# Encoder step on one core: the down projection's operands fetched by product, copied in pairs and subtracted on GpSimd, with spills laid out by pairs

## The chip, the cores and the metric

The kernel runs on one core of a Trainium2 chip. The metric is the device time of one execution in microseconds (us); lower is better. Times of before are the median of three runs.

## The reference, cut to what matters

One layer of a streaming encoder is computed for 592 tokens (16 meta tokens, 512 prompt frames, 64 sample frames): attention in two head groups, an output projection with a residual, and then the part that the change touches, a SwiGLU feed-forward network with a residual and a final norm, in float32, with D_MODEL = 2048 and D_FF = 5632:

```python
x = x + mix @ lp['w_out']
h = rmsnorm(x, lp['norm_ffn_g'])
x = x + (jax.nn.silu(h @ lp['ffn_w_gate']) * (h @ lp['ffn_w_up'])) @ lp['ffn_w_down']
...
y_prompt = rmsnorm(xp[:, N_META:], final_norm_g)
```

## The kernel before

Activations lie transposed: 128 features on the partitions, the 576 tokens that are kept as two halves of QH = 288 columns. Each float32 operand is split in two (`split`, L155): ScalarE (ACT) copies it to a rounded `hi` and VectorE (DVE) subtracts to get `lo`. A product is then three matmuls, hi x hi, hi x lo (both L1089) and lo x hi (L1093).

The feed-forward products run by Strassen-Winograd (`winograd`, L1031): a 2 x 2 block product takes seven products of block sums instead of eight. A *pair* is two chunks of 128 features, so with the two token halves it has four quarters; the seven right-hand operands of a pair are quarters or sums of quarters. For each of the seven products `lhs` (L1067) makes the weight side: products 1, 2 and 4 split a quarter of the raw weights; 5 and 7 need a sum made on GpSimd (POOL), 6 and 3 one made on DVE from an earlier sum (L1058). `split_weights` gives `wh` (ACT, L156) and `wl` (DVE, L153), two buffers each. TensorE (PE) runs the matmuls of all pairs of a block, `take` adds the product to the output on DVE, and `step` lets other work in.

*Gate and up.* 22 turns `u`, each with a gate and an up product over all eight slots of operands (L1243). After each turn GpSimd multiplies the two results (L1278) and, for the first 20 pairs, makes the four sums (L1284 to L1287). The act chunks go to DRAM in `actspill`, the sums in `sumspill`; the DMAs are issued by SP (`load`, `store`).

*Down.* The 22 pairs are taken in blocks of 4, 4, 4, 4, 4 and 2 (L1238). The first five run seven products in the order of `CHAIN` (1, 5, 6, 2, 7, 3, 4) for each of eight turns `d` of 256 output columns; the last runs without sums (`plain_rows`). The output `y` stays in SBUF (16 tiles of 128x576), is first loaded with the residual from `x2spill`, and each product is added to a quarter of it (L1328). While a block runs, `builder` (L1191) prepares the next block's operands in the other four of the eight slots: `fetch` loads a quarter or a sum (144 KB) into `lo`, four loads ahead; ACT copies it to `hi` (L1218), DVE subtracts in place (L1220). Each `step`, so each product, takes one of these two operations: 56 in a block of 56 products. The operands come pair by pair, seven of one pair after another. A separate builder, `start`, prepares the first block at the end of gate/up, by product, and all its copies stand ahead of the first down turn in ACT's program.

Order: SP, ACT, DVE, POOL and PE each run their own queue in order. A scheduler arranges each queue by when it thinks an instruction is ready, except that what `pin` marks (L977, from L1389 on) keeps its place in the program; loads are not marked.

Of the kernel before, what the change touches and what calls it, by code (L numbers as in the profile page):

```python
# [19 lines left out]
P = 128  # L20
# [95 lines left out]
def encoder_step(  # L116
# [195 lines left out]
    x2spill = dp.tile([KC, P, TQ], F32, name="x2spill")  # L312
    actspill = dp.tile([FC, P, TQ], F32, name="actspill")
    sumspill = dp.tile([FC // 2, P, 4, QH], F32, name="sumspill")
# [667 lines left out]

    def operand(m, p, src):
        hi = bc.tile([P, QH], F32R, name=f"bh{p}_{m}")
        lo = bc.tile([P, QH], F32R, name=f"bl{p}_{m}")
        pin(S.activation(hi, src, AF.Copy))
        pin(V.tensor_tensor(lo, src, f32(hi), op=ALU.subtract))
        operands[m, p] = (hi, lo)
# [128 lines left out]
    for i in range(KC):  # L1117
        x = ma.tile([P, TQ], F32, name="x", tag="x", bufs=3)
        load(x, x1spill[i])
        ps = [pmt()[:, 0:QH] for _ in range(2)]  # L1120
        for hf in range(2):
            wh, wl = ws.pop(2 * i + hf)
            for k in range(4):
                mm3(ps, wh[:, k, :], wl[:, k, :],
                    halves(mixh[4 * hf + k]), halves(mixl[4 * hf + k]), hf + k == 0, hf + k == 4)
            fetch(2 * i + hf + 2)
        for xi, pi in zip(halves(x), ps):
            V.tensor_tensor(xi, xi, pi, op=ALU.add)
        xg = ma.tile([P, TQ], F32, name="xg", tag="xg", bufs=2)
        S.activation(xg, x, AF.Copy, scale=gF[:, i:i + 1])  # L1130
        if i == 0:
            G.tensor_tensor(sq2, x, x, op=ALU.mult)
        else:
            G.tensor_tensor(rb2, x, x, op=ALU.mult)
            G.tensor_tensor(sq2, sq2, rb2, op=ALU.add)
        store(x2spill[i], x)
        if i % 2:
            for _ in token_operands(ma, i // 2, xe, xg):
                pass
        xe = xg  # L1140
        if i == 2:
            raw0 = load_raw(rw, w_gate, 0, 8, 0, 1)
# [48 lines left out]
    def builder(m0, count, plain, ahead, by_product=False):  # L1191

        srcs = {}
        for m in range(m0, m0 + count):
            quarter = [actspill[2 * m + f, :, c] for f in range(2) for c in (slice(0, QH), slice(QH, TQ))]
            if plain:
                for p, src in zip((1, 2, 4, 5), quarter):
                    srcs[m, p] = src
            else:
                for p, src in zip(ORDER, (quarter[0], quarter[2], sumspill[m, :, 2], sumspill[m, :, 0],  # L1200
                                          sumspill[m, :, 1], quarter[3], sumspill[m, :, 3])):
                    srcs[m, p] = src
        order = [p for p, _ in CHAIN]
        todo = sorted(srcs, key=lambda mp: order.index(mp[1])) if by_product else list(srcs)

        def fetch(n):
            for m, p in todo[n:n + 1]:
                hi = bc.tile([P, QH], F32R, name=f"bh{p}_{m % 8}")
                lo = bc.tile([P, QH], F32R, name=f"bl{p}_{m % 8}")
                load(f32(lo), srcs[m, p])  # L1210
                operands[m % 8, p] = (hi, lo)

        for n in range(ahead):
            fetch(n)
        for n, (m, p) in enumerate(todo):
            fetch(n + ahead)
            hi, lo = operands[m % 8, p]
            pin(S.activation(hi, f32(lo), AF.Copy))  # L1218
            yield
            pin(V.tensor_tensor(lo, f32(lo), f32(hi), op=ALU.subtract))  # L1220
            yield
# [20 lines left out]
    start = builder(0, blocks[0], False, 4, True)  # L1242
    for u in range(FC // 2):  # L1243
        out = {}
        for which, wsrc in (("g", w_gate), ("u", w_up)):
# [12 lines left out]
            def step():  # L1258
                if u == 0 and which == "u":
                    next(norm, None)  # L1260
                if u == FC // 2 - 1 and which == "u":
                    done[0] += 1
                    if done[0] > 2:
                        for _ in range(2 * blocks[0]):
                            next(start, None)
# [11 lines left out]
        for f in range(2):  # L1277
            G.tensor_tensor(w[:, f, :], w[:, f, :], g[:, f, :], op=ALU.mult)  # L1278
            if u < FC // 2 - 1:
                store(actspill[2 * u + f], w[:, f, :])  # L1280
        if u < FC // 2 - blocks[-1]:
# [6 lines left out]
            store(sumspill[u], t)  # L1288
    for _ in start:
        pass  # L1290
    for f in range(2):
        store(actspill[FC - 2 + f], out["u"][:, f, :])
# [8 lines left out]
    def plain_rows(m0, n, d, hs, slots, done):  # L1301
# [13 lines left out]
        for f in range(2):  # L1315
            for h in hs:
                c = y[2 * d + f][:, h * QH:(h + 1) * QH]
# [3 lines left out]
    def down_rows(m0, n, d, slots, step):  # L1321
        raws = [load_raw(fr, w_down, m0 * 256, 2 * n, d * 256, 2)]
        y11, y12, y21, y22 = quarters(y[2 * d], y[2 * d + 1])
        parts = {1: (y11,), 5: (y22,), 6: (y12,), 2: (y11,), 7: (y22,), 3: (y12,), 4: (y21,)}

        def take(p, banks):
            for c in parts[p]:
                V.tensor_tensor(c, c, banks[p], op=ALU.add)  # L1328
# [6 lines left out]
    def squares(i, h):  # L1335
        c = y[i][:, h * QH:(h + 1) * QH]
# [9 lines left out]
    def finish(h, ahead):  # L1346
# [6 lines left out]
        def turned(q, j):  # L1353
            o, n = tok[h][j]
            ps = pmt()
            for k in range(4):
                PE.transpose(ps[0:n, k * P:(k + 1) * P], y[q * 4 + k][:, o:o + n], ident)  # L1357
# [33 lines left out]
    for bi, n in enumerate(blocks):  # L1391
        slots = [(first + k) % 8 for k in range(n)]
        if bi + 1 < len(blocks):
            build = builder(first + n, blocks[bi + 1], bi + 2 == len(blocks), 4)

            def step():
                next(build, None)

            for d in range(KC // 2):
                if bi == 0:  # L1400
                    for i in (2 * d, 2 * d + 1):
                        y.append(yy.tile([P, TQ], F32, name=f"y{i}"))
                        load(y[i], x2spill[i])
# [93 lines left out]
```

## Time and profile before

| | |
|---|---|
| median of three runs | 2537.51 us (2535.34 to 2537.66) |
| profiled execution, its own time | 2537.73 us |
| its span, first to last instruction | 2535.9 us |
| granted TensorE clock, mean | 0.987 of full speed |
| PE busy | 2421.3 us (95%) |
| DVE busy | 1825.9 us (72%) |
| ACT busy | 1140.9 us (45%) |
| POOL busy | 744.0 us (29%) |
| moved by DMA | 307.70 MB, 121 GB/s |

The seven-product part of down runs from 1974 to 2452 us of the span. Busy PE is not PE at its peak: records of matmuls overlap. PEld is PE's weight load, which runs beside the matmuls; what stands in square brackets behind a row is the idle time just before it and what ended it.

### The profile page before, as it was taken

What the parts mean: (1) busy time and instruction counts of PE and PEld (TensorE: products, weight loads), DVE (VectorE), ACT (ScalarE), POOL (GpSimd) and SP (SyncE); (2) the same over time, 40 slices, a digit from 0 to 9 for tenths busy, and PEclk for the clock granted to TensorE, in tenths of its full rate; (3) what the DMA queues carried; (4) which work ended last, traced back from release to release, by engine and by line L of the source; (5) the groups of instructions that cost most, each with busy time, mean ns of one, the idle gap of its engine ahead of it and who ended that gap; (6) DMA issues with size and microseconds to landing.
All of it is one profiled execution on the core that took longest, in us unless ns stands there. A gap on an engine that the chain in (4) does not pass through costs nothing. (4 is left out here: it accounts for less than half of the span.)

```text
span 2535.9 us, 44403 instructions
## 1 busy us (share of the span) xinstructions
PE 2421.3 (95%) x17607; PEld 2364.8 (93%) x17607; DVE 1825.9 (72%) x2853; ACT 1140.9 (45%) x2064; POOL 744.0 (29%) x601
## 2 busy tenths in 40 slices
PE   6999999998999899999999999999999899999997
PEld 5999999988999888999999999999999899999997
DVE  5466666556555568877777777777777889999975
ACT  5344444343444444444444444444445444444445
POOL 0000000010000165644545444454543222222236
PEclk9999999999999999999999999999999999999999
DMA  6433323343232453333333333333335642542334
GB/s 196 131 94 90 89 81 85 94 135 107 80 102 72 152 156 111 128 128 119 135 101 125 119 124 133 118 120 105 128 128 162 212 149 84 162 152 84 113 98 150
DMA packets 330114, 307.70 MB, mean 121 GB/s; under 512 B 24707, under 2 KB 298506, under 8 KB 329906
## 3 DMA queue, kind: packets, MB, share of 16 engines
q1 hardware_dynamic: 329346, 302.80, 37.8%
q8 instruction: 138, 2.26, 0.4%
q0 software_dynamic: 560, 2.06, 0.2%
q14 instruction: 70, 0.57, 0.1%
HBM read 250.82 MB, written 56.68 MB: 121 GB/s over the span
## 5 line engine op out<-in xcount | busy, mean ns | idle before, releaser
L1089 PE MATMUL m<-bh,wh 128*128 128x288 f32 x3584 | 967.9, 295 | 10.2 <-ACT wh L156 10.2
L1089 PE MATMUL m<-bl,wh 128*128 128x288 f32 x3584 | 967.3, 295 | 0.0
L1089 PEld LDWEIGHTS m<-bh,wh 128*128 128x128 f32 x3584 | 673.6, 188 | 11.1 <-ACT wh L156 11.1
L1089 PEld LDWEIGHTS m<-bl,wh 128*128 128x128 f32 x3584 | 677.2, 189 | 0.1
L1093 PE MATMUL m<-bh,wl 128*128 128x288 f32 x3584 | 586.0, 299 | 16.4 <-DVE wl L153 13.6
L1093 PEld LDWEIGHTS m<-bh,wl 128*128 128x128 f32 x3584 | 511.3, 188 | 31.0 <-DVE wl L153 29.4
L1058 POOL TENSOR_TENSOR ws<-raw 128x512 f32<-128x512 f32 x256 | 344.0, 1352 | 598.6 <-DVE wl L153 321.2
L156 ACT ACTIVATE wh<-ws 128x512 fp32r<-128x512 f32 (+1 forms) x340 | 288.7, 849 | 447.7 <-PE m L1089 303.5
L153 DVE TENSOR_TENSOR wl<-ws,wh 128x512 fp32r<-128x512 f32 (+1 forms) x340 | 384.0, 1129 | 113.4 <-ACT wh L156 113.3
L153 DVE TENSOR_TENSOR wl<-raw,wh 128x512 fp32r<-128x512 f32 x416 | 404.2, 986 | 26.0 <-ACT wh L156 16.8
L156 ACT ACTIVATE wh<-raw 128x512 fp32r<-128x512 f32 x416 | 249.7, 626 | 302.4 <-PE m L1089 282.3
L108 PE MATMUL ps<-xh,wh 128*128 128x296 f32 x992 | 228.3, 312 | 6.8 <-ACT wh L156 6.8
L108 PE MATMUL ps<-xl,wh 128*128 128x296 f32 x992 | 218.8, 302 | 0.0
L108 PE MATMUL ps<-xh,wl 128*128 128x296 f32 x992 | 218.6, 302 | 0.0
L108 PEld LDWEIGHTS ps<-xh,wh 128*128 128x128 f32 x992 | 163.7, 192 | 10.5 <-ACT wh L156 7.0
L108 PEld LDWEIGHTS ps<-xl,wh 128*128 128x128 f32 x992 | 164.0, 192 | 0.0
L108 PEld LDWEIGHTS ps<-xh,wl 128*128 128x128 f32 x992 | 163.6, 191 | 0.3 <-DVE wl L153 0.3
L1058 DVE TENSOR_TENSOR ws<-ws,raw 128x512 f32<-128x512 f32 x128 | 92.2, 721 | 79.4 <-POOL ws L1058 72.1
L153 DVE TENSOR_TENSOR wl<-wr,wh 128x1024 fp32r<-128x1024 f32 (+1 forms) x110 | 117.7, 1070 | 41.4 <-ACT wh L156 39.7
L1328 DVE TENSOR_TENSOR y<-y,m 128x288 f32<-128x288 f32 x280 | 125.3, 447 | 19.2 <-PE m L1093 18.0
L156 ACT ACTIVATE wh<-wr 128x1024 fp32r<-128x1024 f32 (+1 forms) x110 | 101.6, 930 | 71.6 <-PE ps L108 60.9
L1236 POOL TENSOR_TENSOR c<-c,rb 128x576 f32<-128x576 f32 x44 | 73.1, 1662 | 165.0 <-ACT c L1235 165.0
(366 smaller groups left out, 3286.1 us busy)
## 6 DMA issues: line engine op xcount, KB each, us to landing
raw<-in_ffn_w_gate SPq DMA_DIRECT2D x44, 1024.0 KB, 6.7
raw<-in_ffn_w_up SPq DMA_DIRECT2D x44, 1024.0 KB, 6.0
raw<-in_ffn_w_down SPq DMA_DIRECT2D x40, 1024.0 KB, 5.9
wr<-in_w_in SPq DMA_DIRECT2D x60, 512.0 KB, 4.0
actspill<-c SPq DMA_DIRECT2D x44, 288.0 KB, 2.1
sumspill<-c SPq DMA_DIRECT2D x20, 576.0 KB, 2.8
bl<-sumspill SPq DMA_DIRECT2D x80, 144.0 KB, 3.6
bl<-actspill SPq DMA_DIRECT2D x68, 144.0 KB, 4.4
```

What stands on the lines that cost most here:

```text
L108: self.tc.keep_in_program_order(self.pe.matmul(out, lhsT, rhs, start=start, stop=stop))
L153: V.tensor_tensor(lo, src, f32(hi), op=ALU.subtract)
L156: S.activation(hi, src, AF.Copy)
L1058: engine.tensor_tensor(w[:, k:k + m, :], pick(xs), pick(ys), op=op)
L1089: PE.matmul(banks[p], wh[:, k, :], x, start=first and new and k == 0 and x is hi, stop=False, skip_group_check=not new)
L1093: PE.matmul(banks[p], wl[:, k, :], hi, start=False, stop=last and k == n - 1, skip_group_check=not new)
L1236: G.tensor_tensor(g[:, f, :], g[:, f, :], rb2, op=ALU.mult)
L1328: V.tensor_tensor(c, c, banks[p], op=ALU.add)
```

## The change

Operand tiles are joined: for each product and each half of the eight slots one tile [128, 4, 288] for `hi` and one for `lo`. The two spills become one, `pairspill`, with seven pieces of 288 columns for each pair, and a pair's stores are made together (`store_pair`). `builder` now goes by product in the order of `CHAIN`: one load brings the piece of four pairs (576 KB); ACT copies two pairs at once (128x576) and `engine` subtracts two pairs at once. In the down blocks `engine` is GpSimd, for `start` it is still DVE. A step takes an operation only every other product: 28 in a block of 56 products. For the last block, which uses quarters only, four pieces are fetched for two pairs. `y` becomes 8 tiles [128, 4, 288], loaded by one DMA each from `x2spill` in the same layout.

```diff
@@ -309,9 +309,8 @@
 
     xspill = dp.tile([KC, P, TQ], F32, name="xspill")
     x1spill = dp.tile([KC, P, TQ], F32, name="x1spill")
-    x2spill = dp.tile([KC, P, TQ], F32, name="x2spill")
-    actspill = dp.tile([FC, P, TQ], F32, name="actspill")
-    sumspill = dp.tile([FC // 2, P, 4, QH], F32, name="sumspill")
+    x2spill = dp.tile([KC // 2, P, 4, QH], F32, name="x2spill")
+    pairspill = dp.tile([FC // 2, P, 7, QH], F32, name="pairspill")
     mspill = dp.tile([KC, P, TQ], F32, name="mspill")
     trow = dp.tile([H, NREL], F32, name="trow")
     tsk = dp.tile([H, P, NREL], F32, name="tsk")
@@ -980,9 +979,11 @@
 
     pinned = [False]
 
+    rhs_h = {(p, g): bc.tile([P, 4, QH], F32R, name=f"bh{p}{g}") for p in range(1, 8) for g in range(2)}
+    rhs_l = {(p, g): bc.tile([P, 4, QH], F32R, name=f"bl{p}{g}") for p in range(1, 8) for g in range(2)}
+
     def operand(m, p, src):
-        hi = bc.tile([P, QH], F32R, name=f"bh{p}_{m}")
-        lo = bc.tile([P, QH], F32R, name=f"bl{p}_{m}")
+        hi, lo = rhs_h[p, m // 4][:, m % 4], rhs_l[p, m // 4][:, m % 4]
         pin(S.activation(hi, src, AF.Copy))
         pin(V.tensor_tensor(lo, src, f32(hi), op=ALU.subtract))
         operands[m, p] = (hi, lo)
@@ -1133,7 +1134,7 @@
         else:
             G.tensor_tensor(rb2, x, x, op=ALU.mult)
             G.tensor_tensor(sq2, sq2, rb2, op=ALU.add)
-        store(x2spill[i], x)
+        store(x2spill[i // 2, :, 2 * (i % 2):2 * (i % 2) + 2], x.rearrange("p (h c) -> p h c", h=2))
         if i % 2:
             for _ in token_operands(ma, i // 2, xe, xg):
                 pass
@@ -1188,37 +1189,32 @@
 
         return take
 
-    def builder(m0, count, plain, ahead, by_product=False):
-
-        srcs = {}
-        for m in range(m0, m0 + count):
-            quarter = [actspill[2 * m + f, :, c] for f in range(2) for c in (slice(0, QH), slice(QH, TQ))]
-            if plain:
-                for p, src in zip((1, 2, 4, 5), quarter):
-                    srcs[m, p] = src
-            else:
-                for p, src in zip(ORDER, (quarter[0], quarter[2], sumspill[m, :, 2], sumspill[m, :, 0],
-                                          sumspill[m, :, 1], quarter[3], sumspill[m, :, 3])):
-                    srcs[m, p] = src
-        order = [p for p, _ in CHAIN]
-        todo = sorted(srcs, key=lambda mp: order.index(mp[1])) if by_product else list(srcs)
+    PIECE = {1: 0, 2: 1, 3: 2, 5: 3, 6: 4, 4: 5, 7: 6}
+
+    def builder(m0, count, plain, ahead, engine):
+
+        half = m0 % 8 // 4
+        todo = [1, 2, 4, 5] if plain else [p for p, _ in CHAIN]
+        for p in todo:
+            for k in range(count):
+                operands[4 * half + k, p] = (rhs_h[p, half][:, k], rhs_l[p, half][:, k])
 
         def fetch(n):
-            for m, p in todo[n:n + 1]:
-                hi = bc.tile([P, QH], F32R, name=f"bh{p}_{m % 8}")
-                lo = bc.tile([P, QH], F32R, name=f"bl{p}_{m % 8}")
-                load(f32(lo), srcs[m, p])
-                operands[m % 8, p] = (hi, lo)
+            for p in todo[n:n + 1]:
+                piece = {1: 0, 2: 3, 4: 1, 5: 2}[p] if plain else PIECE[p]
+                load(f32(rhs_l[p, half][:, 0:count]),
+                     pairspill[m0:m0 + count, :, piece].rearrange("m p c -> p m c"))
 
         for n in range(ahead):
             fetch(n)
-        for n, (m, p) in enumerate(todo):
+        for n, p in enumerate(todo):
             fetch(n + ahead)
-            hi, lo = operands[m % 8, p]
-            pin(S.activation(hi, f32(lo), AF.Copy))
-            yield
-            pin(V.tensor_tensor(lo, f32(lo), f32(hi), op=ALU.subtract))
-            yield
+            for k in range(0, count, 2):
+                hi, lo = rhs_h[p, half][:, k:k + 2], rhs_l[p, half][:, k:k + 2]
+                pin(S.activation(hi, f32(lo), AF.Copy))
+                yield
+                pin(engine.tensor_tensor(lo, f32(lo), f32(hi), op=ALU.subtract))
+                yield
 
     def token_norm():
         for i in range(2):
@@ -1239,7 +1235,7 @@
 
     turn = 0
     norm = token_norm()
-    start = builder(0, blocks[0], False, 4, True)
+    start = builder(0, blocks[0], False, 2, V)
     for u in range(FC // 2):
         out = {}
         for which, wsrc in (("g", w_gate), ("u", w_up)):
@@ -1261,7 +1257,7 @@
                 if u == FC // 2 - 1 and which == "u":
                     done[0] += 1
                     if done[0] > 2:
-                        for _ in range(2 * blocks[0]):
+                        for _ in range(blocks[0]):
                             next(start, None)
 
             if first:
@@ -1276,8 +1272,15 @@
             gated(g)
         for f in range(2):
             G.tensor_tensor(w[:, f, :], w[:, f, :], g[:, f, :], op=ALU.mult)
-            if u < FC // 2 - 1:
-                store(actspill[2 * u + f], w[:, f, :])
+
+        def store_pair():
+            store(pairspill[u, :, 0], w[:, 0, 0:QH])
+            store(pairspill[u, :, 1:3], w[:, 1, :].rearrange("p (h c) -> p h c", h=2))
+            if u >= FC // 2 - blocks[-1]:
+                store(pairspill[u, :, 3], w[:, 0, QH:TQ])
+
+        if u < FC // 2 - 1:
+            store_pair()
         if u < FC // 2 - blocks[-1]:
             b11, b12, b21, b22 = quarters(w[:, 0, :], w[:, 1, :])
             t = g.rearrange("p f (h c) -> p (f h) c", h=2)
@@ -1285,11 +1288,10 @@
             G.tensor_tensor(t[:, 1, :], b22, t[:, 0, :], op=ALU.subtract)
             G.tensor_tensor(t[:, 2, :], b21, t[:, 1, :], op=ALU.subtract)
             G.tensor_tensor(t[:, 3, :], b22, b12, op=ALU.subtract)
-            store(sumspill[u], t)
+            store(pairspill[u, :, 3:7], t)
     for _ in start:
         pass
-    for f in range(2):
-        store(actspill[FC - 2 + f], out["u"][:, f, :])
+    store_pair()
     close_fb()
     close_rw()
     yy, close_yy = pool("yy", "right")
@@ -1314,18 +1316,17 @@
                         [o[1] for o in ops], g + k == 0, g + k == n + 1)
         for f in range(2):
             for h in hs:
-                c = y[2 * d + f][:, h * QH:(h + 1) * QH]
+                c = y[d][:, 2 * f + h]
                 V.tensor_tensor(c, c, banks[f, h], op=ALU.add)
                 done(2 * d + f, h)
 
     def down_rows(m0, n, d, slots, step):
         raws = [load_raw(fr, w_down, m0 * 256, 2 * n, d * 256, 2)]
-        y11, y12, y21, y22 = quarters(y[2 * d], y[2 * d + 1])
-        parts = {1: (y11,), 5: (y22,), 6: (y12,), 2: (y11,), 7: (y22,), 3: (y12,), 4: (y21,)}
+        y11, y12, y21, y22 = (y[d][:, i] for i in range(4))
+        parts = {1: y11, 5: y22, 6: y12, 2: y11, 7: y22, 3: y12, 4: y21}
 
         def take(p, banks):
-            for c in parts[p]:
-                V.tensor_tensor(c, c, banks[p], op=ALU.add)
+            V.tensor_tensor(parts[p], parts[p], banks[p], op=ALU.add)
 
         winograd(yp, yp, raws, slots, take, step=step, chain=CHAIN)
 
...
@@ -1391,16 +1393,17 @@
     for bi, n in enumerate(blocks):
         slots = [(first + k) % 8 for k in range(n)]
         if bi + 1 < len(blocks):
-            build = builder(first + n, blocks[bi + 1], bi + 2 == len(blocks), 4)
+            build = builder(first + n, blocks[bi + 1], bi + 2 == len(blocks), 4, G)
+            turns = iter(range(1000))
 
             def step():
-                next(build, None)
+                if next(turns) % 2:
+                    next(build, None)
 
             for d in range(KC // 2):
                 if bi == 0:
-                    for i in (2 * d, 2 * d + 1):
-                        y.append(yy.tile([P, TQ], F32, name=f"y{i}"))
-                        load(y[i], x2spill[i])
+                    y.append(yy.tile([P, 4, QH], F32, name=f"y{d}"))
+                    load(y[d], x2spill[d])
                 down_rows(first, n, d, slots, step)
             for _ in build:
                 pass
```

## Rows read from the trace of the kernel before

**Rows 1.** The page's first part: busy time, share of the span and instructions of each engine.

```profile
PE 2421.3 (95%) x17607; PEld 2364.8 (93%) x17607; DVE 1825.9 (72%) x2853; ACT 1140.9 (45%) x2064; POOL 744.0 (29%) x601
```

**Rows 2.** Lines by form, 1978 to 2380 us: busy us, mean ns, idle before, releasers.

```profile
L1093 PEld LDWEIGHTS m<-bh,wl 128*128 128x128 f32 x940 | 137.2, 188 | 25.6 <-DVE wl L153 24.4
```

**Rows 3.** Timeline of PE's weight loads without a wait: start, us, instructions.

```profile
2098.31 0.59 PEld L1093 LDWEIGHTS m<-bh,wl 128*128 128x128 f32 x4
2099.90 0.59 PEld L1093 LDWEIGHTS m<-bh,wl 128*128 128x128 f32 x4
```

**Rows 4.** Timeline of SP, operand loads: second block first and last, fifth block first.

```profile
2059.05 0.82 SPq L137 DMA_DIRECT2D bl<-actspill  x2
...
2078.62 0.43 SPq L137 DMA_DIRECT2D bl<-sumspill  x1
...
2348.36 6.36 SPq L137 DMA_DIRECT2D bl<-actspill  x6
```

**Rows 5.** Waits, 1974 to 2070 and 2070 to 2166 us: total, times, longest.

```profile
PEld m L1093 <- DVE wl L153: 3.9, 9, 0.8
...
PEld m L1093 <- DVE wl L153: 6.7, 12, 1.0
```

**Rows 6.** Timeline around one GpSimd sum, DVE, POOL and PEld.

```profile
2104.96 1.30 POOL L1058 TENSOR_TENSOR ws<-raw 128x512 f32<-128x512 f32 x1 [2.81 <-DVE wl L153]
2105.10 1.71 DVE L153 TENSOR_TENSOR wl<-raw,wh 128x512 fp32r<-128x512 f32 x1
2106.73 0.44 DVE L1328 TENSOR_TENSOR y<-y,m 128x288 f32<-128x288 f32 x1
2106.86 0.56 PEld L1093 LDWEIGHTS m<-bh,wl 128*128 128x128 f32 x4 [0.36 <-DVE wl L153]
2107.10 0.45 DVE L1220 TENSOR_TENSOR bl<-bl,bh 128x288 fp32r<-128x288 f32 x1
2107.47 0.68 DVE L153 TENSOR_TENSOR wl<-raw,wh 128x512 fp32r<-128x512 f32 x1
2108.07 0.44 DVE L1328 TENSOR_TENSOR y<-y,m 128x288 f32<-128x288 f32 x1
```

**Rows 7.** The same, one turn later.

```profile
2116.54 1.29 POOL L1058 TENSOR_TENSOR ws<-raw 128x512 f32<-128x512 f32 x1 [2.82 <-DVE wl L153]
2116.68 1.47 DVE L1220 TENSOR_TENSOR bl<-bl,bh 128x288 fp32r<-128x288 f32 x1
2118.81 0.56 PEld L1093 LDWEIGHTS m<-bh,wl 128*128 128x128 f32 x4 [0.73 <-DVE wl L153]
```

**Rows 8.** Lines by form, 2384 to 2452 us.

```profile
L1093 PEld LDWEIGHTS m<-bh,wl 128*128 128x128 f32 x168 | 24.7, 188 | 0.5 <-DVE wl L153 0.3
L1328 DVE TENSOR_TENSOR y<-y,m 128x288 f32<-128x288 f32 x43 | 19.3, 449 | 7.2 <-PE m L1093 7.2
L1220 DVE TENSOR_TENSOR bl<-bl,bh 128x288 fp32r<-128x288 f32 x2 | 0.9, 451 | 0.0
```

**Rows 9.** GpSimd's 128x576 product in gate/up, by its source line: min/median/max ns.

```profile
L1236 POOL TENSOR_TENSOR c<-c,rb x44: 1427/1700/2412, 1018.4 to 1949.1; 128x576 f32<-128x576 f32 x44
```

**Rows 10.** Timeline: an operand copy on ACT, and a first GpSimd sum.

```profile
2097.58 0.43 ACT L1218 ACTIVATE bh<-bl 128x288 fp32r<-128x288 f32 x1
...
2112.43 1.29 POOL L1058 TENSOR_TENSOR ws<-raw 128x512 f32<-128x512 f32 x1 [6.17 <-DMA raw<-in_ffn_w_down]
```

**Rows 11.** PE, ACT and SP timelines at the change of stage; windows (last: clock, DMA, GB/s).

```profile
1974.01 0.61 PE L1089 MATMUL m<-bh,wh 128*128 128x288 f32 x1 [7.63 <-ACT wh L156]
...
1971.88 1.56 ACT L1218 ACTIVATE bh<-bl 128x288 fp32r<-128x288 f32 x4 [5.05 <-DMA bl<-sumspill]
...
1967.50 1.84 SPq L140 DMA_DIRECT2D actspill<-c  x2
...
1962.00:1964.00 2.00, 2.00 (x17) 2.00 (x17) 2.00 (x6) 0.79 (x2) 0.00 (x0) 1.00 0.99 300
...
1972.00:1974.00 2.00, 0.00 (x0) 0.00 (x0) 1.65 (x7) 2.00 (x6) 0.00 (x0) 0.50 0.75 226
```

More of the change, by code (lines that the diff above doesn't have):

```diff
@@ L1335, in squares @@
     def squares(i, h):
-        c = y[i][:, h * QH:(h + 1) * QH]
+        c = y[i // 2][:, i % 2 * 2 + h]
         if i == 0:
@@ L1356, in turned @@
             for k in range(4):
-                PE.transpose(ps[0:n, k * P:(k + 1) * P], y[q * 4 + k][:, o:o + n], ident)
+                i = q * 4 + k
+                PE.transpose(ps[0:n, k * P:(k + 1) * P], y[i // 2][:, i % 2 * 2 + h, o - h * QH:o - h * QH + n], ident)
             return ps
```

## The prediction

> **What bounds the kernel now.** I read the page's engine shares first: PE is busy 95% of the span, DVE 72%, ACT 45% [rows 1]. That is an average, so I went on to the stage that the change is aimed at, the five down blocks of four pairs that use seven products. The grouped lines of that stage show what PE waits for: the weight loads of the third matmul group (L1093) sat idle 25.6 us, 24.4 of them for DVE's `wl` split [rows 2]. Nothing else holds PE there. The pace without a wait is one product every 1.59 us [rows 3], so a block of 8 turns x 7 products has a floor of 56 x 1.59 = 89.0 us. The operand loads of the second and the fifth block start 289.3 us apart, three blocks, 96.4 us each [rows 4]: 7.4 us over the floor. The list of waits has 6.7 us of them under `wl`, against 3.9 us in the first block [rows 5], which I put at 7.4 x 3.9 / 6.7 = 4.3 us over.
>
> What makes `wl` late is seen in the timeline. GpSimd's weight sum starts at 2104.96; DVE's `wl`, started at 2105.10, is recorded with 1.71 us, and PE then misses 0.36 us. The same `wl` takes 0.68 us two operations later [rows 6]. One turn on, the blocked operation is a `bl` subtract (1.47 us instead of 0.45) and PE misses 0.73 us [rows 7]. The add `y<-y,m`, which reads PSUM, shows no such stretch. So a GpSimd operation and a DVE operation with two SBUF inputs exclude each other. The 1.71 us less the normal 0.68, counted from GpSimd's start, put the exclusion at 1.17 us of a 1.29 to 1.30 us record.
>
> The stage holds a control of its own: after 2384 the last seven-product block has only two `bl` subtracts left, and its L1093 loads idle 0.5 us in 68 us, while DVE waits 7.2 us for PE [rows 8]. Without operand work on DVE, PE runs at its floor.
>
> **The change, term by term.** *Removed from DVE.* In the first four down blocks 28 `bl` subtracts each leave DVE. If nothing took their place, these blocks would fall to the pace of rows 8: 3 x 7.4 + 4.3 = 26.5 us less some 0.5 us per 68 us (3 us over four blocks): **-23.5 us**. This is the whole prize; bounds are 0 and the 26.5 us.
>
> *Added to GpSimd.* Fourteen subtracts of 128x576 per block, 1.75 per turn, beside two sums. The shortest GpSimd operation of this size took 1.43 us [rows 9]; with the same 0.13 us at its end free of exclusion it blocks DVE for 1.30 us. Bounds for the 56: all hidden, 0 us; all passed on to PE in full, 56 x 1.30 = 73 us. To place it I walk the DVE queue. From start to start, a `y` add takes 0.37, a `bl` subtract 0.37 and a `wl` 0.60 us [rows 6], and a weight sum I take like `wl`. Per product DVE has one `y` and one `wl`, 0.97 of 1.59 us, and in two of seven products a sum as well, 1.58 us. I call B the time of a product's `y` add. A copy starts there, 0.73 us before the next product's L1093 loads (2097.58 against 2098.31) [rows 3, 10], so the `wl` of the slot must end by B + 0.73 + 1.59, less about 0.1 for the signal: B + 2.2. GpSimd's first sum starts when the raw weights land, beside the third product's add [rows 10]; its second as soon as the sixth product's `wl` has freed a buffer.
>
> The walk reproduces the kernel before: with four `bl` subtracts in a turn PE misses 0.77 us, with three 0.41; the trace has 0.73 and 0.36 [rows 6, 7]. Now the new queue. A subtract may start 0.65 us after B of the product of its copy, but stands on GpSimd behind sums that were queued earlier. Over four turns the seven copies fall once on each of the seven products. Worst is the third product: the sum blocks to B + 1.16, `wl` runs to 1.76, the subtract holds to 3.06, DVE's own sum ends at 3.67, the next `y` and `wl` at 4.64, that is 3.05 after their own B: PE misses 0.85 us; the second sum then adds 0.4 us, 1.25 together. The second product gives the same, since its subtract waits behind that sum. The fourth and fifth cost 0.36 each, the sixth 0.44, the seventh 0.12. The first costs 0.04 if it is queued ahead of the sum, 1.25 if behind. That is 3.8 or 5.0 us per four turns; I take the middle, 4.4, since no row decides the order. Eight such rounds: **+35 us**. Down blocks together: +11.5 us, with the trace's habit of turning one miss into a later raw load left out on both sides.
>
> *A page on this.* The Trainium skill, "SBUF — State Buffer", section "SBUF: two separate sides", says that the port pair shared by VectorE and GpSimd is locked for the whole instruction. By the rows it is 1.17 of 1.29 us. By the page the price would be 0.13 us more per blocked subtract, and the sum 5 us more, an estimate; it speaks against this change either way.
>
> *The fifth block* builds operands for two pairs: four GpSimd subtracts for eight of DVE, early in the block. 0, with 1 us either way.
>
> *Copies.* ACT makes 14 of 128x576 instead of 28 of 128x288 (0.43 us [rows 10]) per block: the same elements in half the instructions, on an engine that is 45% busy [rows 1], so 0. What hides a copy's wait for its load is the turn (11.1 us) by which a block's first loads go out ahead of it; without it the copy would hold ACT's next `wh` behind it.
>
> *Transfers.* SP issues 7 loads of 576 KB instead of 28 of 144 KB: the same bytes. Now the 28 go out within 20 us (2059.05 to 2078.62 [rows 4]); with 7 they can go out as fast as PE frees each product (590 KB per 1.59 us). Raw loads are queued behind at most one more of them. 0; bounds -2 and +4 us over the four boundaries. The spills of gate/up become 144 + 288 + 576 KB per pair, 144 KB less, in a stretch where PE waits for nothing of theirs; the residual comes in 8 loads instead of 16. 0 each.
>
> *From gate/up to down.* Here PE stands 7.63 us: the last four copies stand in front of the first `wh` on ACT and wait 5.05 us for their loads, and SP had two spill stores between the loads [rows 11]. The granted clock is 0.50 when PE returns (1.2 GHz). Now the last product needs one load and two copies, but SP, which paced 144 KB each, may put all of the next block's earlier products ahead in the same queues, at 300 GB/s [rows 11]. Best case: the first `wh` is ordered ahead of those copies and most of the wait and the slow matmuls after it go, -8; worst: 1.6 MB more ahead, 5 us, less the SP waits, +3. I take **-3**, nearer to the middle. DVE's 14 subtracts here stay on DVE and cost no more than the 28.
>
> Sum: -23.5 + 35 - 3 = +8.5 us on the profiled execution's 2537.7 us (span 2535.9), which stands 0.2 us above the median: **2546 us**.
>
> **Rivals.** *The subtracts fall into DVE's pauses.* The place is the second and third product of a turn. After the relief DVE waits for PE in the first two products (7.2 us in 68 us [rows 8]), and the exclusion is free beside a `y` add. If the subtracts of the second and third copies run there instead of behind the sum, the round costs 1.9 instead of 4.4 us: -23.5 + 15 - 3 = -11.5, **2526 us**. It decides once a round costs less than 2.7 us. For it: DVE loses 14 x 2 x 0.37 = 10.3 us of work per block. Against it: the sums' order in the trace.
>
> *The first down turn starts early.* The walk holds, but the wait between the stages goes: -23.5 + 35 - 8 = +3.5, **2541 us**, within 0.2%. For: four copies become two, and one load replaces four. Against: 300 GB/s are already being moved there.
>
> *GpSimd's order.* A subtract that is queued ahead of a sum and waits for its copy holds up the sum, then ACT's split and PE, for up to 1.4 us; in half of the 32 turns that is +22 over the forecast, **2568 us**. Against: copies run two products ahead.
>
> *Exclusion to the end of the record*, the page's rule above as a mechanism here: 1.43 instead of 1.30 us for some 40 subtracts, +5: **2551 us**. The blocked `wl` of rows 6 speaks against it.
>
> **Numbers.** Forecast 0.38, pauses 0.36, early start 0.19, order 0.05, long exclusion 0.02. A measurement of this kernel can tell about 0.2%, 5 us, from no change. Faster 0.36, same 0.19, slower 0.45. The range runs from 2517 (pauses together with the early start, and a little more) to 2557 us (5.0 us per round and the worst between the stages: -23.5 + 40 + 3); the likeliest case alone spans 2542 to 2554.
>
> **What would show it.** In the profile after: many `wl` still recorded with 1.5 us or more though no `bl` is left on DVE; L1093 loads idle 30 us or more in the down blocks; GpSimd's subtracts right behind its sums; blocks of 97 to 98 us. If the L1093 idle falls under 15 us and DVE shows pauses, the walk's placing was wrong and the first rival holds. A first `wh` before the last copies would show the second; DVE's sum waiting for GpSimd more than now, the third.

## The result, and the profile after

The changed kernel takes 2544.8 us (median of 12 runs, 2540.4 to 2547.6) against 2537.5 us for the kernel before in runs beside it: a ratio of 1.003, 95% interval 1.0022 to 1.0038. That is 7.3 us slower; 2546 us had been forecast.

First the page's engine shares of the changed kernel; they answer to [rows 1].

```profile
PE 2435.9 (96%) x17607; PEld 2376.9 (93%) x17607; DVE 1827.4 (72%) x2719; ACT 1132.8 (45%) x1990; POOL 851.0 (33%) x661
```

GpSimd is busy 107 us more. DVE has 134 instructions fewer and not less busy time: what it lost in work came back as blocked time. PE is busy 14.6 us more with the same 17607 matmuls, and nothing in the prediction accounts for that.

To see where the time lies I cut both profiled executions at events that both have: the first seven-product matmul, PE's longest pause between the stages, and the last `y` add of each block, each by its start (so the pause holds the last matmul's 0.3 us). Times are us.

| | until gate/up | gate/up | pause | blocks 1 to 5 | rest | span |
|---|---|---|---|---|---|---|
| before | 975.2 | 990.9 | 7.9 | 96.9, 96.8, 96.3, 96.2, 91.2 | 84.6 | 2535.9 |
| after | 973.4 | 996.7 | 4.3 | 103.4, 99.4, 95.7, 97.0, 92.2 | 81.8 | 2544.1 |

Blocks 1 to 4 cost 9.3 us more, gate/up 5.8 us more, the pause 3.6 us less. The first and the last column differ by a few us between executions of one and the same code there: 969.9 to 974.4 and 81.8 to 85.0 in the changed kernel and the three kernels below that keep its tiles. So I put nothing on them.

**Down blocks.** The grouped lines by form for the same stretch as [rows 2], 1978 to 2380 us, of the changed kernel (L1094 was L1093 before, L1216 was L1220):

```profile
L1094 PEld LDWEIGHTS m<-bh,wl 128*128 128x128 f32 x919 | 136.1, 190 | 28.2 <-DVE wl L153 27.9
L153 DVE TENSOR_TENSOR wl<-raw,wh 128x512 fp32r<-128x512 f32 x99 | 117.8, 1190 | 0.0
L1329 DVE TENSOR_TENSOR y<-y,m 128x288 f32<-128x288 f32 x229 | 102.3, 447 | 19.9 <-PE m L1094 19.5 <-DMA y<-x2spill 0.2
L1216 POOL TENSOR_TENSOR bl<-bl,bh 128x576 fp32r<-128x576 f32 x57 | 101.6, 1782 | 58.3 <-ACT bh L1214 58.2
```

PE's third group still waits for `wl`, 28.2 us where it was 25.6. No `bl` subtract is left on DVE here, and yet a `wl` of raw weights takes 1190 ns on average, far from the 0.68 us of [rows 6] and more than the 853 ns of the kernel before, whose lines for the same stretch are

```profile
L153 DVE TENSOR_TENSOR wl<-raw,wh 128x512 fp32r<-128x512 f32 x100 | 85.3, 853 | 0.0
L1220 DVE TENSOR_TENSOR bl<-bl,bh 128x288 fp32r<-128x288 f32 x117 | 78.5, 671 | 0.0
```

DVE lost those 78.5 us of subtracts, and its `wl` splits and sums together grew from 233.8 to 304.9 us. DVE has pauses (19.9 us ahead of the `y` adds), so it is not short of time; it is held at the wrong moments. The waits by block, after the change, answer to [rows 5]: 1974 to 2070 us, then 2070 to 2166.

```profile
PEld m L1094 <- DVE wl L153: 8.9, 13, 2.7
...
PEld m L1094 <- DVE wl L153: 7.7, 19, 0.9
```

The timeline around one GpSimd sum shows the mechanism that [rows 6] and [rows 7] showed, now twice in a row:

```profile
2099.50 1.29 POOL L1059 TENSOR_TENSOR ws<-raw 128x512 f32<-128x512 f32 x1 [1.84 <-PE m L1090]
2099.64 1.70 DVE L153 TENSOR_TENSOR wl<-raw,wh 128x512 fp32r<-128x512 f32 x1
2100.75 1.87 POOL L1216 TENSOR_TENSOR bl<-bl,bh 128x576 fp32r<-128x576 f32 x1
2101.39 0.56 PEld L1094 LDWEIGHTS m<-bh,wl 128*128 128x128 f32 x4 [0.36 <-DVE wl L153]
2101.63 1.54 DVE L153 TENSOR_TENSOR wl<-raw,wh 128x512 fp32r<-128x512 f32 x1
2103.22 0.56 PEld L1094 LDWEIGHTS m<-bh,wl 128*128 128x128 f32 x4 [0.22 <-DVE wl L153]
...
2108.54 1.87 POOL L1216 TENSOR_TENSOR bl<-bl,bh 128x576 fp32r<-128x576 f32 x1
...
2109.22 1.74 DVE L1059 TENSOR_TENSOR ws<-ws,raw 128x512 f32<-128x512 f32 x1
...
2111.98 0.56 PEld L1094 LDWEIGHTS m<-bh,wl 128*128 128x128 f32 x4 [0.76 <-DVE wl L153]
```

The subtract is queued right behind the sum. The sum blocks one `wl` (1.70 us), the subtract the next (1.54 us), and PE misses 0.36 and 0.22 us. Eight microseconds on, a subtract blocks DVE's own sum (1.74 us), the `wl` behind that is late, and PE misses 0.76 us. The subtract's record of 1.87 us holds a wait too: the `wl` ended at 2101.34, and the subtract 1.28 us later.

**Loads.** SP's operand loads, first of each block (answering to [rows 4]), show five transfers of 576 KB while the last turn of the block before runs, and two when it is over.

```profile
2066.54 6.97 SPq L137 DMA_DIRECT2D bl<-pairspill  x5
2077.49 1.13 SPq L137 DMA_DIRECT2D bl<-pairspill  x2
```

**Between gate/up and down.** Timelines of PE, ACT, DVE and GpSimd after the change; they answer to [rows 11].

```profile
1974.50 0.61 PE L1090 MATMUL m<-bh,wh 128*128 128x288 f32 x1 [4.05 <-ACT wh L156]
...
1979.18 1.33 PE L1094 MATMUL m<-bh,wl 128*128 128x288 f32 x4 [2.40 <-DVE wl L153]
...
1972.67 1.26 ACT L1214 ACTIVATE bh<-bl 128x576 fp32r<-128x576 f32 x2 [1.73 <-DMA bl<-pairspill]
...
1973.39 3.34 DVE L1216 TENSOR_TENSOR bl<-bl,bh 128x576 fp32r<-128x576 f32 x2 [0.16 <-ACT bh L1214]
...
1976.67 1.86 DVE L1059 TENSOR_TENSOR ws<-ws,raw 128x512 f32<-128x512 f32 x1
...
1972.58 3.53 POOL L1059 TENSOR_TENSOR ws<-raw 128x512 f32<-128x512 f32 x2
1976.07 1.91 POOL L1216 TENSOR_TENSOR bl<-bl,bh 128x576 fp32r<-128x576 f32 x1
```

The windows behind that, again of the changed kernel (the last three columns are the granted clock, the DMA share and GB/s):

```profile
1978.00:1980.00 2.00, 0.81 (x3) 0.82 (x4) 1.90 (x4) 0.63 (x1) 0.00 (x0) 0.50 1.03 403
1980.00:1982.00 2.00, 2.00 (x11) 2.00 (x10) 1.68 (x3) 0.00 (x0) 0.61 (x1) 0.50 1.02 374
1982.00:1984.00 2.00, 2.00 (x11) 2.00 (x11) 0.57 (x2) 0.63 (x1) 0.66 (x1) 0.61 1.05 390
```

ACT's wait for its last load fell from 5.05 to 1.73 us and PE's pause from 7.63 to 4.05. But two `start` subtracts, two sums and the first GpSimd subtract now meet: DVE's first `wl` of the stage is late, and PE stands 2.40 us more in its third group. The GpSimd subtract is the smaller part of that: PE's same wait is 1.80 us in the kernel below that leaves these subtracts out, and 1.40 us in the one that has them on DVE. The granted clock stays at 0.50 (1.2 GHz) into the window from 1982; in the kernel before, whose PE came back at nearly the same time and didn't stop again, the window from 1978 has 0.87 already:

```profile
1978.00:1980.00 2.00, 2.00 (x15) 2.00 (x15) 0.85 (x3) 0.63 (x1) 1.30 (x1) 0.87 0.97 325
```

**Gate/up.** The timeline of PE's weight loads at the end of gate/up, where PE waits for nothing; a row is the third group of one product of 24 matmuls. Before:

```profile
1958.63 1.13 PEld L1093 LDWEIGHTS m<-bh,wl 128*128 128x128 f32 x8
1961.82 1.13 PEld L1093 LDWEIGHTS m<-bh,wl 128*128 128x128 f32 x8
```

After:

```profile
1965.87 1.14 PEld L1094 LDWEIGHTS m<-bh,wl 128*128 128x128 f32 x8
1969.08 1.14 PEld L1094 LDWEIGHTS m<-bh,wl 128*128 128x128 f32 x8
```

One product takes 3.19 us before and 3.21 us after. Averaged over the products from 1100 to 1850 us it is 3.193 against 3.213 us; the stage has 44 x 7 = 308 of them, and 308 x 0.020 = 6.2 us, the size of the 5.8 us. The windows show the same in the middle of the stage; the first count in brackets is PE's matmuls in 100 us, with PE busy all the time and a granted clock of 1.00. Before:

```profile
1100.00:1200.00 100.00, 100.00 (x754) 100.00 (x753) 72.72 (x82) 44.23 (x66) 49.81 (x36) 1.00 0.38 126
```

After:

```profile
1100.00:1200.00 100.00, 100.00 (x749) 100.00 (x748) 72.51 (x83) 43.58 (x66) 49.48 (x36) 1.00 0.38 126
```

So two theories stood to be tested: that the down blocks pay for GpSimd's subtracts, and that the joined operand tiles by themselves slow PE, with where the operands lie in SBUF as the suspect.

### The profile page after: what moved, and what is told of

Its sections match the earlier page's. It is cut to its first block, busy times and chain, and to the rows that moved or that the text cites. A ratio compares the mean times of both kernels' runs of the same rounds, so it can differ in the third digit from the quotient of the medians.

```text
span 2544.1 us, 44111 instructions
## 1 busy us (share of the span) xinstructions
PE 2435.9 (96%) x17607; PEld 2376.9 (93%) x17607; DVE 1827.4 (72%) x2719; ACT 1132.8 (45%) x1990; POOL 851.0 (33%) x661
## 5 line engine op out<-in xcount | busy, mean ns | idle before, releaser
L1094 PE MATMUL m<-bh,wl 128*128 128x288 f32 x3584 | 588.5, 300 | 16.3 <-DVE wl L153 12.6
L1094 PEld LDWEIGHTS m<-bh,wl 128*128 128x128 f32 x3584 | 517.4, 190 | 32.7 <-DVE wl L153 32.2
L153 DVE TENSOR_TENSOR wl<-ws,wh 128x512 fp32r<-128x512 f32 (+1 forms) x340 | 392.3, 1154 | 116.9 <-ACT wh L156 113.7
L153 DVE TENSOR_TENSOR wl<-raw,wh 128x512 fp32r<-128x512 f32 x416 | 436.0, 1062 | 26.9 <-ACT wh L156 15.9
L1059 DVE TENSOR_TENSOR ws<-ws,raw 128x512 f32<-128x512 f32 x128 | 110.7, 866 | 71.6 <-POOL ws L1059 64.2
```

The source lines that it names most:

```text
L1059: engine.tensor_tensor(w[:, k:k + m, :], pick(xs), pick(ys), op=op)
L1094: PE.matmul(banks[p], wl[:, k, :], hi, start=False, stop=last and k == n - 1, skip_group_check=not new)
```

## The experiments

All ratios are to the kernel before, run beside each on the same chip. That kernel's median went from 2535.05 to 2537.5 us between the sets of runs, so kernels of different sets are compared by their ratios, turned into us at 2536 us (0.001 is 2.5 us); each ratio is uncertain by about 0.0009, and a difference of two by somewhat more. Lengths of stages and blocks come from one execution of each kernel. Lines of the code shift by a few from kernel to kernel.

**Joined tiles alone** (the kernel before):

```diff
+    rhs_h = {(p, g): bc.tile([P, 4, QH], F32R, name=f"bh{p}{g}") for p in range(1, 8) for g in range(2)}
+    rhs_l = {(p, g): bc.tile([P, 4, QH], F32R, name=f"bl{p}{g}") for p in range(1, 8) for g in range(2)}
...
-        hi = bc.tile([P, QH], F32R, name=f"bh{p}_{m}")
-        lo = bc.tile([P, QH], F32R, name=f"bl{p}_{m}")
+        hi, lo = rhs_h[p, m // 4][:, m % 4], rhs_l[p, m // 4][:, m % 4]
...
```

> The kernel before with nothing changed but the operand tiles: one tile of 128x4x288 for each product and half of the slots, as in the change. In the two profiles so far PE is never idle in gate/up, yet a product of 24 matmuls takes 3.195 us before and 3.215 us after; 308 such products are the 5.6 us that the change loses there. Theory 1, the place of the operands in SBUF sets that pace: gate/up products at 3.215 us here too, total +5 to +7 us (about 2543 us), down blocks at 96 to 97 us as before. Rival, the pace belongs to the execution or to something else in the change: 3.195 us per product and 2537 us within 2 us.

Measured: 2542.0 us, ratio 1.0022 (1.0013 to 1.003). Gate/up 996.7 us, 3.213 us a product, pause 7.6, blocks 98.5, 97.1, 95.5 and 96.6. The tiles alone bring the slower pace, with every copy, subtract and load as before. Their windows row:

```profile
1100.00:1200.00 100.00, 100.00 (x749) 100.00 (x748) 72.43 (x82) 43.58 (x66) 49.70 (x36) 1.00 0.39 129
```

**Subtracts back on DVE, in pairs** (the changed kernel):

```diff
-            build = builder(first + n, blocks[bi + 1], bi + 2 == len(blocks), 4, G)
+            build = builder(first + n, blocks[bi + 1], bi + 2 == len(blocks), 4, V)
```

> The changed kernel with the down blocks' subtracts on DVE again (two pairs at once, 14 per block), everything else as in the change. Theory of the prediction, that a GpSimd subtract excludes DVE's two-input operations: DVE gets 14 x 0.67 = 9.4 us per block back instead of the 10.3 us of before, L1094 loads idle about as before (6 to 7 us per block), blocks of 96 to 97 us, so within 3 us of the changed kernel, and no wl blocked by a subtract. Rival, the move to GpSimd is what gains in the middle blocks and the loss lies elsewhere: blocks of 98 us and more, 5 us or more slower than the changed kernel.

Measured: 2535.16 us, ratio 0.9995 (0.9987 to 1.0004), 0.0035 or 8.9 us under the changed kernel. Blocks 99.5, 95.9, 94.3, 95.2. PE's third group waits 20.9 us (lines by form, 1978 to 2380 us):

```profile
L1094 PEld LDWEIGHTS m<-bh,wl 128*128 128x128 f32 x943 | 139.7, 190 | 20.9 <-DVE wl L153 19.7
```

The miss is mine: I had expected the two engines to come out nearly level. For pairs GpSimd is the dearer place by about 9 us.

**Subtracts on GpSimd in the kernel before,** one pair at a time:

```diff
...
-            pin(V.tensor_tensor(lo, f32(lo), f32(hi), op=ALU.subtract))
+            pin(engine.tensor_tensor(lo, f32(lo), f32(hi), op=ALU.subtract))
...
-            build = builder(first + n, blocks[bi + 1], bi + 2 == len(blocks), 4)
+            build = builder(first + n, blocks[bi + 1], bi + 2 == len(blocks), 4, engine=G)
```

> The kernel before with only the engine of the down blocks' subtracts changed to GpSimd: 28 of 128x288 per block instead of 14 of 128x576. Exclusion theory: 28 operations hold longer in sum than 14 (each has its own start, about 0.2 us), so the blocks get longer than before, 98 us or more, total +5 to +12 us; the pace in gate/up stays at 3.195 us per product, since the operand tiles are as before. Rival, the subtracts fit into DVE's pauses: blocks of 92 to 95 us, total -6 to -15 us.

Measured: 2534.92 us, ratio 0.9995 (0.9986 to 1.0003). Blocks 100.0, 97.5, 96.5, 96.2 and gate/up 991.0 us. The first blocks of this one profile are longer by 4 us in all, the median is not: in the kernel before, single subtracts cost the same on either engine within the interval. The 5 to 12 us that I expected are not there, so in that kernel the move to GpSimd alone does not cost 9 us.

**No subtract in the down blocks** (the changed kernel; the `lo` operands of blocks 2 to 6 stay unsplit, so that part of the computation is left out):

```diff
-                pin(engine.tensor_tensor(lo, f32(lo), f32(hi), op=ALU.subtract))
+                if engine is V:
+                    pin(engine.tensor_tensor(lo, f32(lo), f32(hi), op=ALU.subtract))
```

> The changed kernel with the subtracts of the down blocks left out (lo keeps the whole operand there; the subtracts of the first block stay): this leaves out part of the computation. It prices the subtracts themselves. Theory of the prediction: without them the blocks fall to about 90 us (floor 89.0 plus what DVE's sums cost), 6 to 7 us per block less than the changed kernel, 24 to 28 us in all: about 2518 us. Rival, the loads or the copies are what costs: blocks stay over 94 us.

Measured: 2524.07 us, ratio 0.9949 (0.9936 to 0.9961). Blocks 95.5, 91.8, 91.8, 92.0; PE's third group idles

```profile
L1094 PEld LDWEIGHTS m<-bh,wl 128*128 128x128 f32 x984 | 145.7, 189 | 5.9 <-DVE wl L153 5.1
```

in the same lines. This splits my two large terms. Against it, the changed kernel's blocks 1 to 4 are 395.5 - 371.1 = 24.4 us longer: the price on GpSimd. Against the kernel before it has 386.2 - 371.1 = 15.1 us less: the prize. The profiled execution is the shortest of only four (2520.1 us), so both sizes are rough; by the ratios of the whole runs the price is 0.0081, 20.5 us.

**The joined order, in separate tiles** (the kernel before):

```diff
...
+    for p in range(1, 8):
+        for g in range(2):
+            for m in range(4 * g, 4 * g + 4):
+                tiles[p, m, "h"] = bc.tile([P, QH], F32R, name=f"bh{p}_{m}")
...
-        hi = bc.tile([P, QH], F32R, name=f"bh{p}_{m}")
-        lo = bc.tile([P, QH], F32R, name=f"bl{p}_{m}")
+        hi, lo = tiles[p, m, "h"], tiles[p, m, "l"]
...
```

and the same loops again for all `lo` behind all `hi`.

> The kernel before, with its operand tiles of 128x288 kept apart, but set out in SBUF in the order that the joined tiles have: all hi of product 1 for the eight slots, then of product 2 and so on, and behind them all lo. Theory 1 (where the operands lie sets the spacing of PE's matmuls): a gate/up product of 24 matmuls takes 3.21 us instead of 3.19, gate/up about 996.7 us, the whole about 2542 us as with joined tiles. Rival (that tiles are joined, with what the program then tracks, sets it): 3.19 us, 991 us and 2536.5 us as before.

Measured: 2541.71 us, ratio 1.0027 (1.0017 to 1.0037), 3.213 us a product, blocks 96.5, 96.7, 96.5, 95.9. Its windows row has the counts of the joined tiles:

```profile
1100.00:1200.00 100.00, 100.00 (x749) 100.00 (x748) 73.10 (x82) 43.21 (x65) 49.20 (x37) 1.00 0.37 121
```

In gate/up nothing but the place of the operands differs from the kernel before, so the place is the cause of the slower pace.

**The changed kernel with subtracts on DVE, and the old place:** one tile for each half, by pair, by product, `lo` right behind `hi`.

```diff
-    rhs_h = {(p, g): bc.tile([P, 4, QH], F32R, name=f"bh{p}{g}") for p in range(1, 8) for g in range(2)}
-    rhs_l = {(p, g): bc.tile([P, 4, QH], F32R, name=f"bl{p}{g}") for p in range(1, 8) for g in range(2)}
+    half_t = [bc.tile([P, 4, 14, QH], F32R, name=f"b{g}") for g in range(2)]
+    place = {p: 2 * i for i, p in enumerate((1, 2, 5, 6, 4, 3, 7))}
+    rhs_h = {(p, g): half_t[g][:, :, place[p]] for p in range(1, 8) for g in range(2)}
+    rhs_l = {(p, g): half_t[g][:, :, place[p] + 1] for p in range(1, 8) for g in range(2)}
```

> The changed kernel with the down blocks' subtracts on DVE, in pairs, and the operands of each half in one tile that sets them out as the kernel before does: by pair, by product, lo right behind hi. Copies, subtracts and loads of several pairs then step through SBUF in strides. Theory 1 (place): gate/up returns to 3.19 us a product and 991 us, so about 5.7 us less than the same kernel with joined tiles, 2529 to 2530 us. Rival (joining): gate/up stays at 996.7 us or more and the whole at 2535 us.

Measured: 2526.63 us, ratio 0.9969 (0.9959 to 0.9978). Gate/up 990.9 us, 3.193 us a product, blocks 98.6, 95.2, 95.0, 94.1. It is 0.0026 or 6.6 us under the same kernel with joined tiles, of which gate/up has 5.8, and 0.3% faster than the kernel before: the pause is 3.9 us where that has 7.9, and blocks 1 to 4 take 382.9 us where that takes 386.2.

```profile
1100.00:1200.00 100.00, 100.00 (x753) 100.00 (x753) 73.19 (x82) 43.61 (x66) 49.60 (x36) 1.00 0.38 126
```

**Copies and subtracts of one pair** (the changed kernel, still on GpSimd and with its loads; `start` works in single pairs too):

```diff
-            for k in range(0, count, 2):
-                hi, lo = rhs_h[p, half][:, k:k + 2], rhs_l[p, half][:, k:k + 2]
+            for k in range(count):
+                hi, lo = rhs_h[p, half][:, k], rhs_l[p, half][:, k]
...
-                if next(turns) % 2:
-                    next(build, None)
+                next(build, None)
```

> The changed kernel, but every copy and every subtract is of one pair (128x288), one operation per product, the subtracts still on GpSimd. Theory 1 (the length of one 128x576 subtract is what makes GpSimd dear: it blocks DVE for over a microsecond at a time, more than PE's lead): the four blocks come down from 395.5 to about 384 us, as in the kernel before with single subtracts on GpSimd less what block 1 shows, and the whole to 2533 to 2536 us. Rival (GpSimd's share of the subtracts as such, or loads by product): blocks of 96 to 103 us and 2543 to 2546 us as in the changed kernel.

Measured: 2539.46 us, ratio 1.0022 (1.0014 to 1.0031). Blocks 100.8, 96.6, 94.6, 95.1, in all 387.1 against 395.5 us. In this profile the blocks come most of the way that theory 1 asked for. The total does not: its ratio is 0.0008 (2 us) under the changed kernel's, and the two intervals overlap. So the length of a subtract is not shown to be the price, though with single copies and subtracts PE loses its time at other places (the table below). Against the pairs on DVE (0.9995) the single subtracts on GpSimd still cost 0.0027, 6.8 us. Why they cost that here and nothing in the kernel before, where loads and copies go pair by pair, no run shows.

**The change itself in the old place** (subtracts on GpSimd in pairs, the two tiles of two experiments above):

```diff
-    rhs_h = {(p, g): bc.tile([P, 4, QH], F32R, name=f"bh{p}{g}") for p in range(1, 8) for g in range(2)}
+    half_t = [bc.tile([P, 4, 14, QH], F32R, name=f"b{g}") for g in range(2)]
...
+    rhs_h = {(p, g): half_t[g][:, :, place[p]] for p in range(1, 8) for g in range(2)}
...
```

> The changed kernel as it is, subtracts on GpSimd in pairs, with nothing but the operands' place taken from the kernel before (one tile for each half, by pair, by product, lo behind hi). If place and engine are two separate costs that add: gate/up 991 us at 3.19 us a product, blocks as in the changed kernel less 1 to 2 us each for the slower matmuls, 2535 to 2539 us, that is 6 to 9 us below the changed kernel and 9 to 10 us above the same kernel with the subtracts on DVE. Rival (the exclusion of GpSimd only shows because the slower matmuls leave no slack): 2527 to 2530 us, as with DVE.

Measured: 2537.59 us, ratio 1.0008 (0.9999 to 1.0017). Gate/up 990.9 us; blocks 102.0, 98.1, 96.8, 96.1. The two costs add: the place is worth 0.0022 (5.6 us) against the changed kernel, the engine 0.0039 (9.9 us) against the kernel with DVE. The lines by form still show the waits of the changed kernel:

```profile
L1096 PEld LDWEIGHTS m<-b,wl 128*128 128x128 f32 x928 | 135.2, 188 | 25.9 <-DVE wl L153 25.7
```

**A third place,** subtracts on DVE in pairs: one tile for each product, slot behind slot, `lo` right behind `hi`.

```diff
+    near = {p: bc.tile([P, 8, 2, QH], F32R, name=f"b{p}") for p in range(1, 8)}
+    rhs_h = {(p, g): near[p][:, 4 * g:4 * g + 4, 0] for p in range(1, 8) for g in range(2)}
+    rhs_l = {(p, g): near[p][:, 4 * g:4 * g + 4, 1] for p in range(1, 8) for g in range(2)}
```

> The kernel with the subtracts on DVE in pairs and the operands in a third place: one tile for each product, the eight slots one behind the other, lo right behind hi. If a lo right behind its hi is what PE's pace wants: 3.19 us a product or less in gate/up and 2526 to 2529 us. If it is the distance from slot to slot (16128 bytes in the kernel before, 1152 in the joined tiles, 2304 here): a pace of its own, nearer to 3.21 us, and 2532 to 2536 us.

Measured: 2527.11 us, ratio 0.9971 (0.9959 to 0.9982), gate/up 990.9 us, 3.193 us a product, blocks 98.2, 94.0, 94.1, 94.6. The distance from slot to slot is another one, the pace is that of the kernel before; in all three places with 3.193 us a `lo` lies right behind its `hi`, in the one place with 3.213 us (joined or separate tiles) it doesn't.

```profile
1100.00:1200.00 100.00, 100.00 (x753) 100.00 (x753) 73.20 (x83) 43.58 (x66) 49.50 (x36) 1.00 0.39 127
```

## Why the prediction was right or wrong

The total was right within 1.2 us, and the sign with it, but that closeness is luck: misses offset each other. In the two profiles the down blocks, gate/up, the pause and the fifth block add up to 9.3 + 5.8 - 3.6 + 1.0 = 12.5 us; the spans differ by 8.2 and the medians by 7.3 us, since the first and the last column, which scatter by as much, came out 1.8 and 2.8 us shorter.

*Removed from DVE, forecast -23.5 us.* Right in kind, too large: 15.1 us measured. The step that failed is the control. I took 0.5 us of waits per 68 us from the end of the fifth block [rows 8] as what remains without operand work. Without any subtract the blocks still take 91.8 us, where I had counted on 89.0 and 0.75: the two sums of a turn block `wl` by themselves, 5.9 us of idle time in 402 us, and some products ran slower in the joined place. The stretch of [rows 8] has the same sums and lost 0.5 us; it has no copies and no loads for a next block, and which of these matters no run took apart. The first block's excess was sized wrongly too: I took 4.3 us from its waits, and by the starts of PE's weight loads it is 7.3 us.

*Added to GpSimd, forecast +35 us.* Right in kind, too large: 24.4 us measured in the blocks, 20.5 us by the whole runs. Each step of the mechanism is in the timeline above: subtracts right behind sums, two `wl` blocked in a row, more than 1.5 us each. What failed is the walk's placing. PE's time over 1.593 us a product, summed over the eight turns of block 2, by the place of the product in the turn (us, from the starts of PE's weight loads; joined tiles add up to 0.03 us a product):

| place in the turn | 1 | 2 | 3 | 4 | 5 | 6 | 7 | all |
|---|---|---|---|---|---|---|---|---|
| before | 0.0 | 0.0 | 0.0 | 0.0 | 0.2 | 2.7 | 4.6 | 7.5 |
| no subtract | 0.0 | 0.0 | 0.1 | 0.1 | 0.1 | 0.3 | 2.0 | 2.6 |
| after | 1.0 | 1.1 | 0.0 | 0.1 | 0.1 | 4.8 | 3.2 | 10.2 |
| single copies and subtracts, on GpSimd | 0.0 | 0.1 | 0.0 | 0.0 | 0.0 | 4.3 | 2.9 | 7.4 |

I had put the worst at the third and second product and something on the fourth and fifth. They lose next to nothing. In blocks 2 to 4 all 24 second sums start in the sixth product, where PE loses most; 12 of the 42 subtracts start in the seventh and 12 in the first two. The first sums and the other 18 subtracts start in the third to fifth, and what they cost reaches PE later: the subtract of 2108.54 starts in the fifth product and its 0.76 us are missing in the sixth. So the losses fall partly where the kernel before lost time already (the seventh place even gains), and the price was 7.9, 7.6, 3.9 and 5.0 us in the four blocks against my 8.8 in each. With single copies and subtracts the loss in the first two places is gone.

*Down blocks together, forecast +11.5 us:* 9.3 measured. Both terms were 8 to 11 us too large with opposite signs, so the difference held; that is luck.

*Gate/up, forecast 0 for the spills, and nothing at all for the joined tiles.* This is the step that failed outright: +5.8 us. I costed the DMAs of the stage and "a stretch where PE waits for nothing of theirs" was right. I never asked what the new tiles do to PE itself. A stage where PE is never idle has no cover for a slower matmul.

*Between the stages, forecast -3 us:* the pause fell by 3.6 us, by a part of the mechanism named. SP's stores now stand behind the loads instead of between them; the number of copies is not it, since the kernel that copies single pairs has the same pause (4.4 against 4.3 us). But the third group's wait of 2.40 us behind it was not foreseen. The first two places of the turn lost 6.7 us over block 1's eight turns, against 2.0 before, where in block 2 they lost 2.1 and 0.0. So some 2.6 us of the gain was given back at the head of block 1, where it stands among the 9.3. Little of that is GpSimd's: these two places lose 4.8 us without any subtract and 5.1 us with the subtracts on DVE.

*Copies, loads, the fifth block, 0 each:* no copy waited for a load in the blocks. The fifth block was 1.0 us longer, as in the other kernels with this place (92.1 with joined, 92.2 with separate tiles). From the pairs and the loads by product I expected nothing: with subtracts on DVE and the old place the kernel is 7.9 us faster than before by its ratio, so the rest of the change is worth more than the 3 us that I gave it.

*The page.* The Trainium skill, "SBUF — State Buffer", section "SBUF: two separate sides", has the pair of ports locked for the whole instruction. Here the `wl` of 2101.63 ended at 2103.17; less its own 0.68 us it began at 2102.49, 0.13 us before the end of the subtract's record at 2102.62. As in [rows 6] the measured hold is a little shorter than the record, and the measurement decides.

*Rivals.* The pauses did take some of it, but blocks of 95.7 to 103.4 us are not the 2526 us case. The idle time of 28.2 us in the third group lies just under the 30 us that I had named as a sign, far from the 15 us of this rival. An earlier first down turn came and was mostly given back. GpSimd did wait for copies (58.2 us in the lines above), without becoming the bound.

The time from before to after, from the ratios: the place +5.6 to +6.8 us (joined tiles alone, separate tiles, and the two pairs of kernels that differ in the place only), GpSimd instead of DVE for pairs +8.9 to +9.9 (in either place), the rest of the change -7.9 to -7.4 (the two kernels with DVE and a good place). Their sum lies from +6.6 to +9.3 us, and the measured ratio of 1.003 is 7.6 us.

## What to carry to other kernels

When an engine has spare time but excludes the one that feeds PE while it works, count moments, not busy shares: work taken off DVE came back as longer `wl` records. Joining tiles to save instructions changes where operands lie; where PE never idles, look at the spacing of its matmuls before and after. A change with several parts is best run part by part: loads by product and pairs on DVE were a gain here (0.9969 with the old place), and two other parts hid it. Which of the two gained, loads by product or pairs on DVE, was not run apart.

## What was not expected of the hardware

The spacing of matmuls depends on where their moving operands lie in SBUF. The same 24 matmuls, at the granted clock of 1.00 and with PE never idle, take 3.193 us with `lo` right behind `hi` (three layouts) and 3.213 us with all `lo` behind all `hi` (joined or separate), in every product alike. Within a product single spacings differ, 130 to 140 ns in the one and 128 to 146 ns in the other, always at the same matmuls. Of the 20 ns, 16 fall on the sixteen matmuls that alternate `hi` and `lo`, 4 on the eight that read `hi` alone. Why is open; only one place with the slower pace was run, and no run here varied the distances one by one.

Pairs of subtracts (128x576) cost 8.9 to 9.9 us more on GpSimd than on DVE in otherwise the same kernel, in either place, though GpSimd is busy only 33% of the span. Single subtracts in the kernel before cost the same on either engine. On GpSimd, single copies and subtracts against pairs are 2 us apart in the changed kernel, which is not clear of the noise.
